# A two-layer hybrid DiT on one core: most adaLN products on VectorE as dot products, and the feed-forward layer's inner features in two parts

## The chip, the cores and the metric

The kernel runs on one core of a Trainium2 chip. The engines are PE (TensorE, matmuls), DVE (VectorE), ACT (ScalarE), POOL (GpSimd) and SP (SyncE, which issues most of the DMAs). The metric is the device time of one execution in microseconds (us), as the median of several; a single profiled execution gives the trace, whose span is a little shorter than that execution's own time.

## The reference, cut to what matters

Two token streams of 256 tokens each (`x` and `ctx`, width 1024) go through two layers. Each layer is a feed-forward sublayer, a mixer (neighbourhood attention and an SSD branch), and a second feed-forward sublayer. In front of every sublayer the stream is normalised, scaled and shifted, and behind it the result is gated, by nine vectors of 1024 features for each layer and stream. These come from one conditioning vector per stream:

```
def adaln(v, w, b):
    m = jax.nn.silu(v) @ w + b          # v: 1024, w: 1024 x 9216
    return m.reshape(m.shape[:-1] + (N_MOD, D_MODEL))

def ffn_sublayer(s, mod, i, g_norm, w_gate, w_up, w_down):
    h = modulate(rmsnorm(s, g_norm), mod[:, :, i], mod[:, :, i + 1])
    return s + 0.5 * mod[:, :, i + 2] * swiglu(h, w_gate, w_up, w_down)   # D_FF = 2816
```

So adaLN is a product of a 1024 x 9216 matrix per layer with just two vectors. Layer 1 needs no second feed-forward and no mixer output for `ctx`.

## The kernel before, in words

**Layout.** Activations lie with features on the partitions and the 512 tokens of both streams (two segments of 256) in the columns. `self.x[k]` holds the residual stream and `self.h[k]` the normalised input of a sublayer, for 128 features each.

**Weights.** Every weight is used as a high and a low half. `wchunk` loads 512 KB (four blocks of 128 rows by 256 columns) into `raw` (3 buffers) with a DMA issued by SP, ACT casts it (L90), and DVE subtracts to get the low half (L91). Both halves lie in `hl` (4 buffers). `gemm_t` then runs three matmuls for each block of 128 rows (L114 to L116).

**Feed-forward.** `ffn` walks over 11 chunks of 256 inner features. A chunk is 96 matmuls, as a rule of 512 columns: two groups of 24 for gate into `pg`, two for up into `pu`. ACT takes Silu of `pg`, DVE multiplies with `pu` (L371), and the product is split into `act` (ACT L303, DVE L304), 22 tiles in all. The four products rotate over three PSUM banks. Chunk 0 goes segment by segment, so that the norm of segment 1 (`norm`, whose `rstd` is a chain of nine tiny DVE operations, L200 to L208, then `dg` at L222, a matmul L224 into `rbc`, and L248 to L252 into `h`) may run beside segment 0's products. After all chunks `onto_x` multiplies `act` with w_down, four blocks of 256 output features, and `resid` (L298) adds each onto `x`. The last `tail` blocks go segment by segment, so that the norm of segment 0 for the next sublayer may run beside segment 1's products.

**adaLN.** One unit is 256 features of one of the nine kinds: two loads of 512 KB into `wa` (issued by SP), and products of `wa` with the 32-column stationary `cs` on PE (L153). Four units share a PSUM bank; DVE copies it (L157), PE sums it with a selection matrix (L160), and DVE adds the bias (L166 and the lines behind it). There are 72 units. The first 8 run in a start phase ahead of the first feed-forward layer. The generator `ada_all` hands out the other 64 in slots between the products of the first three feed-forward layers: 6 kinds in each of layer 0's two, and 4 in layer 1's first.

**Order.** Each engine works through its own instructions in order. A scheduler at build time places the instructions of `ffn`, so the order is fixed by when it expects an operand and an engine to be free. All weight loads and the adaLN loads stand in the one queue that SP issues.

## Time and profile before

| | before |
|---|---|
| median of 3 runs | 2913.41 us (2911.05 to 2914.53) |
| profiled execution | 2915.16 us |
| its span | 2913.2 us |
| PE busy | 2834.8 us (97%) |
| DVE busy | 1699.7 us (58%) |
| ACT busy | 1339.1 us (46%) |

The stages, read from the timeline: the start phase to 26 us, the first feed-forward layer to 447, the mixer of layer 0 with its output projection (the last 50 us of it) to 1318, the second feed-forward layer to 1719, layer 1's first feed-forward layer to 2114, its mixer to 2690, and its second feed-forward layer, for one stream, to the end. The busy times are sums over the whole span; which engine an instruction waits for in one stage is read from windows and from the waits in them.

### The profile page before, as it was taken

The numbers are of one execution on the slowest core, as the hardware profiler recorded it, in microseconds if no ns is written. First come the engines' busy times: TensorE is split into PE (matmuls) and PEld (weight loads), VectorE is DVE, ScalarE is ACT, GpSimd is POOL, SyncE is SP. The second block draws the span as 40 slices with busy tenths as digits, with TensorE's granted clock in tenths as the row PEclk, the third lists the DMA queues.
The fourth block names the chain that finished last, engine by engine and source line by source line (L and its number), as shares of the span: only waits on it lengthen the run. The fifth ranks groups of instructions, "written<-read, shape, count | busy, mean of one in ns | idle before, by whom it ended". The sixth has DMA issues, their size and how long they took to land.

```text
span 2913.2 us, 42876 instructions
## 1 busy us (share of the span) xinstructions
PE 2834.8 (97%) x16872; PEld 2304.1 (79%) x16872; DVE 1699.7 (58%) x3320; ACT 1339.1 (46%) x2447; POOL 76.7 (3%) x132
## 2 busy tenths in 40 slices
PE   7999998999999999999999999999989999999899
PEld 4777788776776777788777797777888787789899
DVE  4333246677569989765333263332477777899654
ACT  3222223544468878733222142222344457787453
POOL 0000000000000000000000000000001000001000
PEclk9999999999999999999999999999999999999999
DMA  7555554322232222344544544444554343235564
GB/s 255 175 155 158 166 167 104 88 55 55 83 87 63 75 74 87 94 155 138 156 145 148 166 152 144 131 145 137 163 145 74 79 127 88 87 109 168 167 188 152
DMA packets 365737, 371.95 MB, mean 128 GB/s; under 512 B 15456, under 2 KB 358624, under 8 KB 365536
## 3 DMA queue, kind: packets, MB, share of 16 engines
q1 hardware_dynamic: 358112, 349.28, 39.7%
q0 software_dynamic: 7424, 19.93, 3.7%
q8 instruction: 133, 2.18, 0.3%
q14 instruction: 68, 0.56, 0.1%
HBM read 360.77 MB, written 8.39 MB: 127 GB/s over the span
## 4 chain that ended last, share of the span: by engine, by line
PE 88%; DVE 5%; DMA 3%; ACT 3%; issue 1%; POOL 0%; SPq 0%; ACTq 0%; DVEq 0%; POOLq 0%
PE pd L114 5%; PE pd L115 5%; PE pd L116 5%; PE pg L114 5%; PE pg L115 5%; PE pg L116 5%; PE pu L114 5%; PE pu L115 5%; PE pu L116 5%; PE xps L114 3%; PE xps L115 3%; PE xps L116 3%; PE ps_y L809 3%; PE ps_ada L153 3%; PE qkps L125 2%; PE qkps L126 2%
## 5 line engine op out<-in xcount | busy, mean ns | idle before, releaser
L91 DVE TENSOR_TENSOR hl<-raw,hl 128x1024 fp32r<-128x1024 f32 (+1 forms) x538 | 625.9, 1166 | 756.9 <-ACT hl L90 756.0
L90 ACT CAST hl<-raw 128x1024 fp32r<-128x1024 f32 (+1 forms) x538 | 538.5, 1003 | 734.9 <-PE pd L116 283.3
L114 PE MATMUL pd<-act,hl 128*128 128x256 f32 (+1 forms) x836 | 280.6, 336 | 0.0
L115 PE MATMUL pd<-act,hl 128*128 128x256 f32 (+1 forms) x836 | 279.6, 334 | 0.0
L116 PE MATMUL pd<-act,hl 128*128 128x256 f32 (+1 forms) x836 | 278.5, 333 | 0.0
L114 PE MATMUL pg<-h,hl 128*128 128x512 f32 (+1 forms) x736 | 267.1, 364 | 6.2 <-ACT h L303 5.0
L115 PE MATMUL pg<-h,hl 128*128 128x512 f32 (+1 forms) x736 | 265.2, 360 | 0.0
L116 PE MATMUL pg<-h,hl 128*128 128x512 f32 (+1 forms) x736 | 264.8, 360 | 0.0
L114 PE MATMUL pu<-h,hl 128*128 128x512 f32 (+1 forms) x696 | 254.7, 366 | 0.0
L115 PE MATMUL pu<-h,hl 128*128 128x512 f32 (+1 forms) x696 | 253.3, 364 | 0.0
L116 PE MATMUL pu<-h,hl 128*128 128x512 f32 (+1 forms) x696 | 252.7, 363 | 0.0
L125 PE MATMUL qkps<-hl,h 128*128 128x256 f32 x672 | 195.5, 291 | 1.8 <-ACT v L453 1.8
L126 PE MATMUL qkps<-hl,h 128*128 128x256 f32 x672 | 193.3, 288 | 0.9 <-DVE hl L91 0.9
L127 PE MATMUL qkps<-hl,h 128*128 128x256 f32 x672 | 192.0, 286 | 0.0
L114 PEld LDWEIGHTS pd<-act,hl 128*128 128x128 f32 x836 | 157.1, 188 | 23.0 <-issue 4.9
L116 PEld LDWEIGHTS pd<-act,hl 128*128 128x128 f32 x836 | 157.0, 188 | 17.0 <-issue 0.8
L115 PEld LDWEIGHTS pd<-act,hl 128*128 128x128 f32 x836 | 157.0, 188 | 16.6 <-issue 1.2
L114 PEld LDWEIGHTS pg<-h,hl 128*128 128x128 f32 x736 | 138.7, 189 | 38.7 <-issue 7.4
L836 DVE SCALAR_TENSOR_TENSOR m<-m,dtn,cbm 128x256 f32<-128x256 f32 (+1 forms) x384 | 144.6, 412 | 36.1 <-ACT m L834 35.6
L115 PEld LDWEIGHTS pg<-h,hl 128*128 128x128 f32 x736 | 139.1, 189 | 23.9 <-DVE h L304 1.3
L116 PEld LDWEIGHTS pg<-h,hl 128*128 128x128 f32 x736 | 139.1, 189 | 23.0 <-issue 0.8
L114 PEld LDWEIGHTS pu<-h,hl 128*128 128x128 f32 x696 | 131.2, 189 | 28.1 <-issue 6.6
(264 smaller groups left out, 5930.8 us busy)
## 6 DMA issues: line engine op xcount, KB each, us to landing
wa<-in_w_ada_dram SPq DMA_DIRECT2D x144, 512.0 KB, 4.6
raw<-in_w_in_dram SPq DMA_DIRECT2D x144, 512.0 KB, 4.0
raw<-in_ffn_w_down_dram SPq DMA_DIRECT2D x95, 512.0 KB, 3.5
raw<-in_ffn_w_gate_dram SPq DMA_DIRECT2D x88, 512.0 KB, 3.8
raw<-in_ffn_w_up_dram SPq DMA_DIRECT2D x88, 512.0 KB, 3.8
raw<-in_ssd_w_o_dram SPq DMA_DIRECT2D x32, 512.0 KB, 3.5
raw<-in_w_out_dram SPq DMA_DIRECT2D x20, 512.0 KB, 3.5
raw<-in_na_w_o_dram SPq DMA_DIRECT2D x16, 512.0 KB, 3.4
```

Source lines behind the costliest of these rows:

```text
L90: nc.scalar.copy(hl[:, 0], t)
L91: nc.vector.tensor_tensor(out=hl[:, 1], in0=t, in1=hl[:, 0].bitcast(F32), op=ALU.subtract)
L114: mm(ps, wh, xh[:, cols], start=(first and i == 0), stop=False)
L115: mm(ps, wh, xl[:, cols], start=False, stop=False)
L116: mm(ps, wl, xh[:, cols], start=False, stop=(last and i == len(st) - 1))
L125: mm(ps, xh[:, cols], wh, start=(i == 0), stop=False)
L126: mm(ps, xh[:, cols], wl, start=False, stop=False)
L127: mm(ps, xl[:, cols], wh, start=False, stop=(i == len(st) - 1))
L153: mm(ps[32 * j : 32 * j + 32, :256], self.cs[:, k0 + j, 6 - 2 * i : 38 - 2 * i], w[:, j], start=(i + k0 == 0), stop=(i == len(units) - 1 a ...
L809: nc.tensor.matmul(*a, **k)
L836: v.scalar_tensor_tensor(out=e[:, o1], in0=e[:, o1], scalar=self.dtn[:, 2 * s + j, r : r + 1], in1=cbm[s][:, d, o1], op0=ALU.mult, op1=ALU ...
```

## The change

The first two kinds of layer 0 stay on PE in the start phase. The other 16 kinds become dot products on DVE: the host transposes their weights (`w_adt`), so that 128 output features lie on the partitions and the 1024 input features in the columns. For each of 8 blocks of a kind, SP loads 512 KB into `wt` (3 buffers), and two `scalar_tensor_tensor` of 128x1024 (one for each stream) multiply it with the broadcast Silu of the conditioning vector (`cb`) and sum along the row (`accum_out`). That makes 128 loads and 256 such operations. At the start of each of the three feed-forward layers, `cb` (1 MB) is loaded and goes through Silu on ACT. The product itself goes to a scratch tile `junk` that nobody reads.

The inner features of a feed-forward layer are used in two parts: after chunk 5 `onto_x` takes the first 12 blocks of `act`, and after chunk 10 the remaining 10, with the last two instead of the last one of the four output blocks going segment by segment. Each part adds onto `x`, so `resid` runs twice for each output block; `act` has 12 buffers in place of 22. The number of matmuls of the feed-forward layers is unchanged. `cc` and `cs` move into a pool that is closed after the start phase.

```
     def ada_all(self):
-        first = [[(0, m, u) for m in (1, 0)] for u in range(4)]
-        rest = [[(l, m, u) for u in range(4)] for l in range(L) for m in range(9)][2:]
-        for units in first + rest:
-            yield from self.ada_steps(units)
...
+        kinds = [(l, m) for l in range(L) for m in range(9)][2:]
+        def load(i):
+            w = self.wada.tile([P, D], F32, name="wt", tag="wt", bufs=3)
+            nc.sync.dma_start(w, self.I["w_adt"][i // KD, i % KD * P : (i % KD + 1) * P, :])
+            return w
+        for i, (l, m) in enumerate(kinds):
+            md = self.mods[9 * l + m][0]
+            for k in range(KD):
+                w = self.wnext or load(i * KD + k)
+                more = not self.stop_after(l, m, k)
+                self.wnext = load(i * KD + k + 1) if more else None
+                for s in range(2):
+                    nc.vector.scalar_tensor_tensor(out=self.junk, in0=w, scalar=1.0, in1=self.cb[:, s], op0=ALU.mult, op1=ALU.mult,
+                                                   accum_out=md[:, k, s : s + 1])
...
-    def onto_x(self, l, m, w, nk, rhs, nseg, tail, ada=None):
+    def onto_x(self, l, m, w, ka, kb, rhs, nseg, tail, ada=None):
...
-            self.wada, self.nwada, self.nada = fp, 2, 1
+            self.wada = fp
+            if nada:
+                self.cb = fp.tile([P, 2, D], F32, name="cb", tag="cb")
+                self.junk = fp.tile([P, D], F32, name="junk", tag="junk")
...
+                nc.scalar.activation(self.cb, self.cb, AF.Silu)
...
-            nsl = 1 + 2 * (nch - 1) + 9
-            slots = iter([4 * nada * (i + 1) // nsl - 4 * nada * i // nsl for i in range(nsl)])
+            half = (nch + 1) // 2
+            nsl = 1 + 2 * (nch - 1) + 12 + 6
+            slots = iter([KD * nada * (i + 1) // nsl - KD * nada * i // nsl for i in range(nsl)])
...
             for c in range(nch):
+                if c == half:
+                    self.after_seg = None
+                    self.onto_x(l, m + 2, wd, 0, 2 * half, actr, nseg, 0, ada)
...
-                    a = fp.tile([P, 2, T], F32R, name="act", tag="act", bufs=KF)[:, :, cols]
+                    a = fp.tile([P, 2, T], F32R, name="act", tag="act", bufs=2 * half)[:, :, cols]
...
-            self.onto_x(l, m + 2, wd, KF, lambda k: (act[k][:, 0], act[k][:, 1]), nseg, 1, ada)
+            self.onto_x(l, m + 2, wd, 2 * half, KF, actr, nseg, 2, ada)
```

What the build-time order makes of it is shown at three places. The first is DVE's queue in a chunk of the first feed-forward layer. Before, one chunk has four weight subtractions (L91), two products (L371), two splits (L304) and sometimes the copy of a finished bank (L157):

```order
L91 TENSOR_TENSOR hl<-raw,hl 128x1024 x2
L371 TENSOR_TENSOR sg<-pu,sg 128x512
L304 TENSOR_TENSOR act<-sg,act 128x512
L91 TENSOR_TENSOR hl<-raw,hl 128x1024
L371 TENSOR_TENSOR sg<-pu,sg 128x512
L91 TENSOR_TENSOR hl<-raw,hl 128x1024
L304 TENSOR_TENSOR act<-sg,act 128x512
L157 COPY adas<-ps_ada 128x256
```

After, the same work stands there (its lines are now L91, L408 and L331), with the dot products (L192) between:

```order
L192 SCALAR_TENSOR_TENSOR junk,mod_3_104<-wt,cb 128x1024 x2
L91 TENSOR_TENSOR hl<-raw,hl 128x1024
L192 SCALAR_TENSOR_TENSOR junk,mod_3_104<-wt,cb 128x1024 x2
L408 TENSOR_TENSOR sg<-pu,sg 128x512
L192 SCALAR_TENSOR_TENSOR junk,mod_3_104<-wt,cb 128x1024
L331 TENSOR_TENSOR act<-sg,act 128x512
L192 SCALAR_TENSOR_TENSOR junk,mod_3_104<-wt,cb 128x1024
L91 TENSOR_TENSOR hl<-raw,hl 128x1024
L192 SCALAR_TENSOR_TENSOR junk,mod_3_104<-wt,cb 128x1024
L408 TENSOR_TENSOR sg<-pu,sg 128x512
L91 TENSOR_TENSOR hl<-raw,hl 128x1024
L331 TENSOR_TENSOR act<-sg,act 128x512
```

Twelve or thirteen dot products stand in each chunk from 1 to 5, and eight in each of the four w_down blocks of the first part; from chunk 6 on none are left in the feed-forward layers of layer 0 (96 operations in each), and none in layer 1's first (64).

The second place is DVE's queue where the norm of segment 1 ahead of the second feed-forward layer of layer 0 is worked out. Before, the nine steps of the reciprocal root stand in one piece, followed by `dg`:

```order
L200 TENSOR_SCALAR rs_a<-ssq 128x2
L201 TENSOR_SCALAR rs_y<-rs_a 128x2
L202 TENSOR_TENSOR rs_t<-rs_y 128x2
L203 TENSOR_TENSOR rs_t<-rs_t,rs_a 128x2
L204 SCALAR_TENSOR_TENSOR rs_y<-rs_t,rs_y 128x2
L205 SCALAR_TENSOR_TENSOR rs_t<-rs_y 128x2
```

After, a dot product of this layer's kinds stands behind nearly every step (the steps are now L227 to L235, `dg` is L249):

```order
L227 TENSOR_SCALAR rs_a<-ssq 128x2
L192 SCALAR_TENSOR_TENSOR junk,mod_8_109<-wt,cb 128x1024
L228 TENSOR_SCALAR rs_y<-rs_a 128x2
L192 SCALAR_TENSOR_TENSOR junk,mod_8_109<-wt,cb 128x1024
L229 TENSOR_TENSOR rs_t<-rs_y 128x2
L192 SCALAR_TENSOR_TENSOR junk,mod_8_109<-wt,cb 128x1024
L230 TENSOR_TENSOR rs_t<-rs_t,rs_a 128x2
L192 SCALAR_TENSOR_TENSOR junk,mod_8_109<-wt,cb 128x1024
L231 SCALAR_TENSOR_TENSOR rs_y<-rs_t,rs_y 128x2
L192 SCALAR_TENSOR_TENSOR junk,mod_8_109<-wt,cb 128x1024
```

Eight dot products have moved between `rs_a` and `dg` there, and one between `dg` and the normalised tiles; 11 more stand in the output projection ahead of it.

The third place is SP's queue in a chunk of the first feed-forward layer. Before, two `wa` loads stand among the four raw loads of a chunk (two of gate, two of up):

```order
L83 DMA wa<-in_w_ada_dram 128x4x256 x2
L83 DMA raw<-in_ffn_w_gate_dram 128x4x256
L83 DMA raw<-in_ffn_w_up_dram 128x4x256
L83 DMA wa<-in_w_ada_dram 128x4x256 x2
L83 DMA raw<-in_ffn_w_up_dram 128x4x256
L83 DMA raw<-in_ffn_w_gate_dram 128x4x256
```

After, six or seven `wt` loads of the same size stand among them:

```order
L83 DMA raw<-in_ffn_w_gate_dram 128x4x256 x2
L182 DMA wt<-in_w_adt_dram 128x1024 x4
L83 DMA raw<-in_ffn_w_up_dram 128x4x256
L182 DMA wt<-in_w_adt_dram 128x1024
L83 DMA raw<-in_ffn_w_up_dram 128x4x256
L182 DMA wt<-in_w_adt_dram 128x1024 x2
```

The loads of a feed-forward layer's kinds have moved into its first half, where a raw load now stands behind up to four `wt` loads.

## Rows read from the trace of the kernel before

**Rows 1.** The page's first part: PE, its busy time, share and instructions

```profile
PE 2834.8 (97%) x16872; PEld 2304.1 (79%) x16872; DVE 1699.7 (58%) x3320; ACT 1339.1 (46%) x2447; POOL 76.7 (3%) x132
```

**Rows 2.** Windows: stretch, its length, busy time by engine, PEclk, DMA share, GB/s

```profile
0.00:26.00 26.00, 11.51 (x84) 6.13 (x84) 12.63 (x38) 12.72 (x20) 0.20 (x4) 0.97 0.96 318
61.00:311.00 250.00, 250.00 (x1261) 191.35 (x1260) 82.50 (x113) 69.87 (x102) 0.00 (x0) 1.00 0.53 161
```

**Rows 3.** Lines by form, PE: adaLN products, count, busy us, mean ns, idle before

```profile
L153 PE MATMUL ps_ada<-wa,cs 128*32 128x256 f32 x1152 | 82.8, 391 | 0.1
```

**Rows 4.** Timeline of PE around one adaLN unit: start, duration, instruction

```profile
149.70 0.40 PE L116 MATMUL pg<-h,hl 128*128 128x512 f32 x1
...
152.50 0.40 PE L116 MATMUL pg<-h,hl 128*128 128x512 f32 x1
...
158.10 0.40 PE L116 MATMUL pu<-h,hl 128*128 128x512 f32 x1
158.42 1.07 PE L153 MATMUL ps_ada<-wa,cs 128*32 128x256 f32 x16
...
159.76 0.40 PE L115 MATMUL pu<-h,hl 128*128 128x512 f32 x1
```

**Rows 5.** Timeline of PE around one selection matmul group

```profile
194.10 0.40 PE L116 MATMUL pg<-h,hl 128*128 128x512 f32 x1
194.33 0.51 PE L160 MATMUL ps_ada<-c_cst,adas 128*128 128x8 f32 x4
...
195.24 0.39 PE L116 MATMUL pg<-h,hl 128*128 128x512 f32 x1
```

**Rows 6.** Lines by form, DVE: weight subtraction, and operations with two float32 sources

```profile
L91 DVE TENSOR_TENSOR hl<-raw,hl 128x1024 fp32r<-128x1024 f32 x483 | 589.2, 1222 | 710.4 <-ACT hl L90 709.5
L836 DVE SCALAR_TENSOR_TENSOR m<-m,dtn,cbm 128x256 f32<-128x256 f32 x192 | 92.0, 479 | 36.1 <-ACT m L834 35.6
L836 DVE SCALAR_TENSOR_TENSOR m<-m,dtn,cbm 128x128 f32<-128x128 f32 x192 | 66.1, 344 | 0.0
```

**Rows 7.** Timeline of DVE: two independent operations in a row

```profile
64.25 1.22 DVE L91 TENSOR_TENSOR hl<-raw,hl 128x1024 fp32r<-128x1024 f32 x1
65.38 1.28 DVE L304 TENSOR_TENSOR act<-sg,act 128x512 fp32r<-128x512 f32 x2
```

**Rows 8.** Timeline of ACT: an operation with an accumulator, and its read

```profile
559.63 0.70 ACT L518 ACTIVATE p<-ps_s,mx 128x512 f32<-128x512 f32 x1
560.21 0.20 ACT L518 ACTIVATION_READ_ACCUMULATOR p<-ps_s,mx 128x1 f32 x1
560.30 0.69 ACT L518 ACTIVATE p<-ps_s,mx 128x512 f32<-128x512 f32 x1
```

**Rows 9.** Timeline of DVE: segment 1's norm ahead of layer 0's second feed-forward

```profile
1325.18 0.16 DVE L200 TENSOR_SCALAR rs_a<-ssq 128x2 f32<-128x2 f32 x1 [2.38 <-PE ssq L217]
...
1326.95 0.48 DVE L222 TENSOR_SCALAR dg<-c_cst,rs_y 128x128 f32<-128x128 f32 x2
...
1329.29 1.27 DVE L252 SCALAR_TENSOR_TENSOR h<-nh,mod,h 128x256 fp32r<-128x256 f32 x3
```

**Rows 10.** Timeline of PE there: the first matmul of segment 1

```profile
1330.28 0.28 PE L114 MATMUL pg<-h,hl 128*128 128x256 f32 x1
```

**Rows 11.** Timeline of PE behind an idle time: 19 matmuls from 467.67 to 471.65

```profile
466.82 1.20 PE L224 MATMUL rbc<-dg,ones 128*128 128x128 f32 x4 [10.40 <-DVE dg L222]
467.67 0.56 PE L125 MATMUL qkps<-hl,h 128*128 128x256 f32 x1
...
471.65 0.28 PE L125 MATMUL qkps<-hl,h 128*128 128x256 f32 x1
```

**Rows 12.** Waits from 61 to 311 us: who waits for whom, total, times, longest

```profile
ACT hl L90 <- PE pu L116: 40.8, 19, 3.1
DVE sg L371 <- PE pu L116: 35.5, 20, 2.9
```

**Rows 13.** DMA issues of the page: count, KB each, median us to landing

```profile
wa<-in_w_ada_dram SPq DMA_DIRECT2D x144, 512.0 KB, 4.6
```

More of the change, by code (lines that the diff above doesn't have):

```diff
@@ L150, in ada_steps @@
                 w = self.wada.tile([P, 4, 256], F32, name="wa", tag="wa", bufs=self.nwada)
[L151 removed]
+                self.load(w, self.I["w_ada"], k0, 4, m * D + u * 256, 256)
                 for j in range(4):
@@ L173, in ada_all @@
-    def ada_all(self):
-        first = [[(0, m, u) for m in (1, 0)] for u in range(4)]
-        rest = [[(l, m, u) for u in range(4)] for l in range(L) for m in range(9)][2:]
-        for units in first + rest:
-            yield from self.ada_steps(units)
-            self.ada_done = units[0][:2]
-            if self.pause:
+            if m == 1:
+                nc.vector.scalar_tensor_tensor(out=md, in0=md, scalar=1.0, in1=two(PAR["g1"][0] + 2 * u), op0=ALU.add, op1=ALU.mult)
+    def ada_all(self):
+        for u in range(4):
+            yield from self.ada_steps([(0, m, u) for m in (1, 0)])
+            yield
+        self.ada_done = (0, 1)
+        nc = self.nc
+        kinds = [(l, m) for l in range(L) for m in range(9)][2:]
[12 more added lines that the diff above has]
+                                                   accum_out=md[:, k, s : s + 1])
+                if k == KD - 1:
+                    two = lambda n, o: self.pars[l][:, PAR[n][0] + o : PAR[n][0] + o + KD][:, :, None].to_broadcast([P, KD, 2])
+                    nc.vector.tensor_tensor(out=md, in0=md, in1=two("b_ada", m * KD), op=ALU.add)
+                    if m in (1, 4, 7):
+                        nc.vector.scalar_tensor_tensor(out=md, in0=md, scalar=1.0, in1=two({1: "g1", 4: "gm", 7: "g2"}[m], 0),
+                                                       op0=ALU.add, op1=ALU.mult)
+                    elif m in (2, 8):
+                        nc.vector.tensor_scalar(out=md, in0=md, scalar1=0.5, scalar2=None, op0=ALU.mult)
+                    self.ada_done = (l, m)
@@ L180, in ada_all, with stop_after @@
                 yield
+    def stop_after(self, l, m, k):
+        return k == KD - 1 and (l, m) in ((0, 7), (1, 4), (1, 8))
     def mod(self, l, m, k, s):
-        return self.mods[9 * l + m][k // 2][:, k % 2, s : s + 1]
+        return self.mods[9 * l + m][1][k // 2][:, k % 2, s : s + 1]
     def fill(self, n=1):
@@ L312, in onto_x @@
                 continue
-            if ada and split:
-                ada(True)
             for sg in [[s] for s in range(nseg)] if split else [list(range(nseg))]:
@@ L318, in onto_x @@
                     pd = [self.bank("pd")[:, : len(sg) * SEG] for _ in range(2)]
-                    for a in range(0, nk, 4):
-                        ws = self.wcols(w, min(4, nk - a), cc * 256, k0=a)
+                    for a in range(ka, kb, 4):
+                        ws = self.wcols(w, min(4, kb - a), cc * 256, k0=a)
                         for t in range(2):
-                            self.gemm_t(pd[t], ws, t * P, P, rhs, cols, a == 0, a + 4 >= nk)
-                        if ada and not split and a % 8:
+                            self.gemm_t(pd[t], ws, t * P, P, rhs, cols, a == ka, a + 4 >= kb)
+                        if ada and not split:
                             ada()
@@ L335, in ffn @@
         with tc.tile_pool(name="ffn", bufs=1) as fp, tc.tile_pool(name="pph", bufs=1, space=PSUM) as self.pph:
-            self.wada, self.nwada, self.nada = fp, 2, 1
+            self.wada = fp
+            if nada:
+                self.cb = fp.tile([P, 2, D], F32, name="cb", tag="cb")
+                self.junk = fp.tile([P, D], F32, name="junk", tag="junk")
+                nc.sync.dma_start(self.cb.rearrange("p s k -> p (s k)"),
+                                  self.I["c2"].rearrange("s k -> (s k)")[None, :].to_broadcast([P, 2 * D]))
+                nc.scalar.activation(self.cb, self.cb, AF.Silu)
             act = []
             nch = DFF // 256
-            nsl = 1 + 2 * (nch - 1) + 9
-            slots = iter([4 * nada * (i + 1) // nsl - 4 * nada * i // nsl for i in range(nsl)])
+            half = (nch + 1) // 2
+            nsl = 1 + 2 * (nch - 1) + 12 + 6
+            slots = iter([KD * nada * (i + 1) // nsl - KD * nada * i // nsl for i in range(nsl)])
             def ada(end=False):
-                self.pause = end
-                self.fill(1 if end and nada else next(slots, 0))
+                self.fill(KD * nada if end else next(slots, 0))
+            actr = lambda k: (act[k][:, 0], act[k][:, 1])
             for c in range(nch):
+                if c == half:
+                    self.after_seg = None
+                    self.onto_x(l, m + 2, wd, 0, 2 * half, actr, nseg, 0, ada)
                 if pre and c == 0:
@@ L1004, in body @@
                 if l == 0 and m < 2:
-                    K.mods.append([cp.tile([P, 2, 2], F32, name=f"mod{m}_{u}") for u in range(4)])
+                    K.mods.append((None, [cp.tile([P, 2, 2], F32, name=f"mod{m}_{u}") for u in range(4)]))
                 else:
-                    t = cp.tile([P, 4, 2, 2], F32, name=f"mod{l}_{m}")
-                    K.mods.append([t[:, u] for u in range(4)])
+                    t = cp.tile([P, KD, 2], F32, name=f"mod{l}_{m}")
+                    K.mods.append((t, [t[:, 2 * u : 2 * u + 2] for u in range(4)]))
         K.pars = [cp.tile([P, NPAR], F32, name=f"par{l}") for l in range(L)]
-        nc.sync.dma_start(cc, I["cc"])
         K.load_con("cst", cp)
```

26 lines of the change are left out of this document (12 added, 14 removed).

## The prediction

> **What bounds the kernel now.** I read the engine line first [rows 1]: PE is busy 97% of the span, DVE 58%. That is an average, so I then read the windows of the stages that the change touches. From 61 to 311 us, inside the first feed-forward layer, PE is busy in all of its 250 us and DVE in 82.5 [rows 2], a third. The reader is to see there that every microsecond of PE work which leaves such a stage shortens it, as long as the work that takes its place fits into DVE's other two thirds. The waits of the same stretch say what DVE and ACT do meanwhile: ACT's weight casts wait for PE to give back a weight buffer (19 waits, 40.8 us), and DVE's product waits for PE's `pu` (20 waits, up to 2.9 us) [rows 12]. Both run ahead of PE. The start phase is the opposite: 318 GB/s with the DMA engines busy 0.96 of the time, and PE busy 11.5 of 26 us [rows 2]; the change leaves its work as it is.
>
> **What PE loses.** The adaLN products are 1152 recorded matmuls, 16 for each of 72 units [rows 3]. Their mean of 391 ns is no price, since they overlap. I take it from the timeline. Two 512-column matmuls of the same kind stand 12 places apart at 149.70 and 152.50, so one place is 0.233 us [rows 4]. Around one unit the starts go from 158.10 to 159.76, 1.66 us, with two ordinary places in it: 1.66 - 2 x 0.233 = 1.19 us for a unit. For a selection group it is 195.24 - 194.10 = 1.14 us with three ordinary places: 0.44 us [rows 5]. 64 units and 16 groups leave: 64 x 1.19 + 16 x 0.44 = 76.2 + 7.0 = **83.2 us**. All of it lies in the three feed-forward layers, where PE is the bound. The two-part sum over inner features costs PE nothing in itself, since the matmuls are the same in number.
>
> **What DVE gains: the price of one dot product.** No operation of DVE with an accumulator is in the trace, so I bound it. Multiplications of the same form with two float32 sources take 479 ns for 256 columns and 344 for 128 [rows 6]: 1.055 ns a column, hence 479 + 768 x 1.055 = 1.29 us for 1024. An independent operation starts before the one ahead has ended: 1.22 us long, but the next start 1.13 later [rows 7], so 1.29 becomes a pitch of 1.20. That is the lower end, an accumulator that costs nothing. A dependent operation follows later: nine steps of the root take 1326.95 - 1325.18 = 1.77 us, 0.197 each for a duration of 0.16 [rows 9], 0.04 more than the duration. Two dot products in a row both write `junk` and so wait for one another: 1.33. ACT's accumulator is read by an instruction of its own, which makes the pitch 0.09 longer: 0.70 us long, the next start 0.67 later, where its read starts after 0.58 (559.63, 560.21, 560.30 in [rows 8]). With that the upper end is 1.42. I take the middle, **1.35 us**, as the order has both pairs in a row and single ones between other work. 256 x 1.35 = 346 us of DVE, in stages where it has more than twice that free; but the order puts them in the first halves.
>
> [...]
>
> **Does it fit?** In chunks 1 to 5 the order gives DVE 12 or 13 dot products, four subtractions (1.13 each) and four operations of 0.6 [rows 7]: 13 x 1.35 + 4.5 + 2.4 = 24.5 us, against PE's 96 x 0.233 = 22.4. With 1.20 it would be 22.5, just even; with 1.42 it is 25.4. So DVE falls behind by 0 to 3 us a chunk, 0 to 15 over five chunks. In the w_down blocks of the first part it is about even (72 x 0.233 = 16.8 us of PE; 8 x 1.35 + 3 x 1.13 + 4 x 0.48 = 16.1 of DVE). PE doesn't notice at once: the four products of a chunk rotate over three banks, so DVE's reading of a bank may come two products late, 2 x 24 x 0.233 = 11.2 us. The upper end thus exceeds the cover by 4 us in each of layer 0's two layers; layer 1's first has 64 dot products, about 10 a chunk, and fits. There is a second path: an SP queue in order, in which a raw load stands behind up to four `wt` loads, and each of these waits for one of three buffers that only DVE frees. Whenever DVE is late, the next raw load is late too, and a load takes 4.6 us to land [rows 13]. I charge one and a half landings for each of layer 0's two layers and one half for layer 1's: 3.5 x 4.6 = 16, an estimate, and take **+15 us** for both paths. Ends: 0, if the cover holds; 40, if it fails from the first chunk (two layers x 5 x 3, and half as much for layer 1's and the queue). All other DVE work of the change is small: 16 additions of 128x16, and 40 additions onto `x` of 0.48 [rows 6], beside 16.8-us blocks; the copies of adaLN banks go.
>
> **Where it can't fit: the norm of segment 1.** Ahead of layer 0's second feed-forward layer, PE needs segment 1's `h` at 1330.28 [rows 10], and the first one is being written from 1329.29 [rows 9], about 0.6 us of slack. The order now has eight dot products between `rs_a` and `dg`. Nothing else is queued on PE between segment 0's products and `rbc`, which waits for `dg`. So the chain grows by 8 x 1.35 less the gaps they fill (some 0.3), 10.5 us; the ninth hides mostly under `rbc`. Less 0.6 it is 9.9. Behind an idle time of 10.4 us PE ran 19 matmuls of 256 columns in 3.98 us instead of 19 x 0.117 = 2.2 [rows 11]: 1.8 more. Sum **+12 us**. The ends are 9 (at 1.20) and 13.
>
> **Smaller terms.** Eleven dot products in the output projection are 15 us of DVE, one of them in the root chain of segment 0's norm, with `cb` and its Silu beside them: **+2.5** (0 to 8). The start of the first feed-forward layer, where 1 MB of `cb` (two landings like those of rows 13) joins transfers that were at 318 GB/s [rows 2], 3 us at that rate: **+2** (0 to 5). The turn from w_down back to chunk 6, where PE's next bank waits for `resid`: **+2** (0 to 4, two operations of 0.48 in each of three layers and what they wait for). The blocks that go by segment are now two of 10 in place of one of 22, so what covers the norm of segment 0 falls from 132 to 120 matmuls of half the columns, 15.5 to 14.1 us: nothing, or 1.4 in each of two layers if the cover was just long enough.
>
> **The sum.** -83.2 + 15 + 12 + 2.5 + 2 + 2 = -49.7. The profiled run (2915.2, span 2913.2) lies 1.8 above the median of the three, 2913.4; from the median this is **2864 us**. About 0.2% (6 us) is what a measurement of this kernel can tell from no change.
>
> **The rivals.** *The cover holds.* DVE's price is at the lower end or its lateness stays inside 11.2 us, and only the norm and the turn cost: -83.2 + 9 to 12 + 2 = 2841, 2835 to 2850. For it: DVE and ACT wait for PE now [rows 12]. Against it: the order fills DVE to the brim.
>
> *The queue binds.* DVE is at 1.42 and SP's queue passes its lateness to the raw loads: 40 in place of 15, so 2889, 2880 to 2905. If it takes yet 20 more, the gain is spent, and the time is within 0.2%.
>
> [...]
>
> **How the numbers follow.** Forecast 0.47; cover holds 0.18; queue binds 0.20; within 0.2% 0.03; half rate 0.12. Own range of the forecast 2848 to 2882. The range reaches from 2838, which holds most of the first rival, to 2905, the end of the queue's: 0.47 + 0.15 + 0.20, about 8 in 10. Faster by over 0.2% is 0.47 + 0.18 + 0.20 = 0.85, within it 0.03, slower 0.12.
>
> **What the profile after would show.** Right: no `ps_ada` matmuls behind the start phase, PE's busy time down by about 83 us, dot products of 1.29 us (plus a second short instruction) at a pitch of 1.3 to 1.4, PE idle for some 10 us before `rbc` at the second feed-forward layer, and idle times of PE in chunks 3 to 5 and the first w_down blocks, released by DVE's `hl` or by a bank. Wrong: dot products of over 2 us (half rate), or PE without any idle time in the first halves (cover holds), or idle times of which the releaser is a DMA (queue).

## The result, and the profile after

The changed kernel takes 2844.9 us (median; 2843.8 to 2852.3), against 2914.0 us for the kernel before on the same chip: a ratio of 0.9769 (95% interval 0.9757 to 0.9780), 69 us faster. That lies inside the predicted range (2838 to 2905) but not inside the forecast's own (2848 to 2882). It is the time of the first rival, the cover that holds (2835 to 2850); the predicted range reached down to 2838 to hold most of that rival.

The page's first part of the changed kernel answers to [rows 1]:

```profile
PE 2752.6 (97%) x15748; PEld 2274.6 (80%) x15748; DVE 2007.0 (71%) x3793; ACT 1344.2 (47%) x2453; POOL 76.9 (3%) x132
```

PE has lost 82 us of busy time (2834.8 before), the span 69.2 (2913.2 before, 2844.0 after, both of the profiled executions). DVE has gained 307. The lines by form say where PE's loss comes from; they answer to [rows 3] (columns: line, engine, operation, shapes, count; then busy us and mean ns; then idle time before):

```profile
L153 PE MATMUL ps_ada<-wa,cs 128*32 128x256 f32 x128 | 11.2, 426 | 0.0
...
L160 PE MATMUL ps_ada<-c_cst,adas 128*128 128x8 f32 x16 | 2.1, 242 | 0.5 <-DVE adas L157 0.5
```

Of 72 units the 8 of the start phase are left, 128 recorded matmuls in place of 1152. What takes their place on DVE is a `scalar_tensor_tensor` and, as an instruction of its own, the accumulator's read (lines by form, DVE; the second row is other work, an addition of 256 columns):

```profile
L192 DVE SCALAR_TENSOR_TENSOR junk<-wt,cb 128x1024 f32<-128x1024 f32 x256 | 312.5, 1221 | 7.8 <-DMA wt<-in_w_adt_dram 3.4 <-ACT cb L367 0.2
...
L263 DVE TENSOR_TENSOR ssacc<-ssacc,sst 128x256 f32<-128x256 f32 x99 | 41.3, 419 | 2.8 <-ACT sst L262 1.4
...
L192 DVE DVE_READ_ACCUMULATOR junk<-wt,cb 128x1 f32 x256 | 20.8, 81 | 0.0
```

One dot product lasts 1.22 us, and its read 0.08. The prediction's extrapolation had 1.29.

Where the 69 us went is read by stage. The bounds are the starts of the first matmul of each stage in PE's timeline, in the profiled executions, in us:

| stage | before | after | difference |
|---|---|---|---|
| start phase, to the first gate product | 26.3 | 25.6 | -0.7 |
| layer 0's first feed-forward layer | 419.5 | 386.7 | -32.8 |
| mixer of layer 0 | 823.0 | 822.9 | -0.1 |
| output projection, second feed-forward layer, layer 1's first | 844.0 | 804.9 | -39.1 |
| mixer of layer 1 | 570.5 | 571.6 | +1.1 |
| last projection and last feed-forward layer | 223.0 | 224.5 | +1.5 |
| end | 6.9 | 7.8 | +0.9 |

By the prediction's prices the first feed-forward layer should lose 24 x 1.19 + 6 x 0.44 = 31.2 us of PE, and it lost 32.8. The fourth row should lose 40 x 1.19 + 10 x 0.44 = 52.0 and lost 39.1: 12.9 us stayed there.

The windows say why the first layer lost all of it (columns as in [rows 2]: stretch, length, busy time of PE, PEld, DVE, ACT, POOL, then PEclk, DMA share and GB/s). They are its chunks 1 to 5, its first part of w_down, and its chunks 6 to 10:

```profile
61.00:176.00 115.00, 115.00 (x507) 93.00 (x506) 112.26 (x173) 39.29 (x68) 0.00 (x0) 1.00 0.79 255
176.00:243.00 67.00, 67.00 (x289) 54.27 (x288) 60.48 (x97) 13.15 (x13) 0.00 (x0) 1.00 0.66 207
243.00:355.00 112.00, 112.00 (x481) 90.18 (x480) 36.92 (x40) 31.11 (x39) 0.00 (x0) 1.00 0.30 90
```

In chunks 1 to 5 DVE is busy 112.3 of 115 us, and PE all the same 115 of 115. The forecast's idle times of PE aren't there.

DVE falls behind a little, though. Its first product of three successive chunks (timeline of DVE, start and duration) starts at:

```profile
126.05 0.68 DVE L408 TENSOR_TENSOR sg<-pu,sg 128x512 f32<-128x512 f32 x1
...
148.95 0.69 DVE L408 TENSOR_TENSOR sg<-pu,sg 128x512 f32<-128x512 f32 x1
...
171.93 0.69 DVE L408 TENSOR_TENSOR sg<-pu,sg 128x512 f32<-128x512 f32 x1
```

22.90 and 22.98 us apart, against 22.4 of PE: DVE loses half a microsecond a chunk, 3 us over five chunks, where by the prediction's estimate 11.2 us may be lost. The waits from 61 to 243 us answer to [rows 12]:

```profile
ACT hl L90 <- PE pd L116: 45.4, 10, 4.5
ACT act L330 <- DVE sg L408: 25.8, 6, 5.6
...
ACT hl L90 <- DMA raw<-in_ffn_w_gate_dram: 2.4, 1, 2.4
...
DVE sg L408 <- PE pu L116: 0.3, 1, 0.3
```

In [rows 12] DVE's product waited 20 times for PE's `pu`, 35.5 us in all, in a stretch that is a third longer. Of that wait 0.3 us are left, once: DVE now comes after PE. But PE itself is in no row of the list; it waits for nobody. ACT's casts still wait for PE, and the loads held them up once, for 2.4 us.

### The profile page after: what moved, and what is told of

Its sections match the earlier page's. It is cut to its first block, busy times and chain, and to the rows that moved or that the text cites. A ratio compares the mean times of both kernels' runs of the same rounds, so it can differ in the third digit from the quotient of the medians.

```text
span 2844.0 us, 41229 instructions
## 1 busy us (share of the span) xinstructions
PE 2752.6 (97%) x15748; PEld 2274.6 (80%) x15748; DVE 2007.0 (71%) x3793; ACT 1344.2 (47%) x2453; POOL 76.9 (3%) x132
## 4 chain that ended last, share of the span: by engine, by line
PE 85%; DVE 6%; DMA 4%; ACT 3%; issue 1%; POOL 0%; SPq 0%; ACTq 0%; DVEq 0%; POOLq 0%
PE pg L115 5%; PE pg L114 5%; PE pg L116 5%; PE pd L116 5%; PE pd L115 5%; PE pd L114 5%; PE pu L115 5%; PE pu L116 5%; PE pu L114 5%; PE xps L114 3%; PE xps L115 3%; PE xps L116 3%; PE ps_y L846 3%; PE qkps L125 2%; PE qkps L127 2%; PE qkps L126 2%
## 5 line engine op out<-in xcount | busy, mean ns | idle before, releaser
L91 DVE TENSOR_TENSOR hl<-raw,hl 128x1024 fp32r<-128x1024 f32 (+1 forms) x538 | 624.1, 1162 | 468.0 <-ACT hl L90 466.5
L192 DVE SCALAR_TENSOR_TENSOR junk<-wt,cb 128x1024 f32<-128x1024 f32 x256 | 312.5, 1221 | 7.8 <-DMA wt<-in_w_adt_dram 3.4
L116 PE MATMUL pd<-act,hl 128*128 128x512 f32 (+1 forms) x824 | 277.3, 336 | 0.0
L115 PE MATMUL pd<-act,hl 128*128 128x512 f32 (+1 forms) x824 | 276.6, 336 | 0.0
L114 PE MATMUL pd<-act,hl 128*128 128x512 f32 (+1 forms) x824 | 276.1, 335 | 0.0
L115 PEld LDWEIGHTS pd<-act,hl 128*128 128x128 f32 x824 | 154.8, 188 | 18.1
L114 PEld LDWEIGHTS pd<-act,hl 128*128 128x128 f32 x824 | 154.9, 188 | 17.9
L116 PEld LDWEIGHTS pd<-act,hl 128*128 128x128 f32 x824 | 155.0, 188 | 16.5
```

The lines of the kernel that those rows point to most:

```text
L91: nc.vector.tensor_tensor(out=hl[:, 1], in0=t, in1=hl[:, 0].bitcast(F32), op=ALU.subtract)
L114: mm(ps, wh, xh[:, cols], start=(first and i == 0), stop=False)
L115: mm(ps, wh, xl[:, cols], start=False, stop=False)
L116: mm(ps, wl, xh[:, cols], start=False, stop=(last and i == len(st) - 1))
L192: nc.vector.scalar_tensor_tensor(out=self.junk, in0=w, scalar=1.0, in1=self.cb[:, s], op0=ALU.mult, op1=ALU.mult, accum_out=md[:, k, s : s ...
```

## The experiments

The theory after the result: the 83 us of adaLN matmuls are gone in full; inside the chunks the dot products cost nothing, since DVE has just the time for them; what is lost again is lost in the norm of segment 1 at layer 0's second feed-forward layer. The rivals: the two parts of the inner features gave or took some of it; the transfers cost; or DVE is late after all and PE pays somewhere else.

### No dot product in the norm, nor in the output projection ahead of it

The place is seen in PE's timeline of the changed kernel, with the idle time before each instruction in brackets:

```profile
1286.28 0.50 PE L114 MATMUL pg<-h,hl 128*128 128x256 f32 x2 [1.54 <-ACT h L278]
...
1303.91 1.19 PE L251 MATMUL rbc<-dg,ones 128*128 128x128 f32 x4 [5.51 <-DVE dg L249]
1306.21 0.80 PE L114 MATMUL pg<-h,hl 128*128 128x256 f32 x2 [1.11 <-ACT h L278]
```

and in DVE's, which answers to [rows 9]:

```profile
1293.21 0.15 DVE L227 TENSOR_SCALAR rs_a<-ssq 128x2 f32<-128x2 f32 x1
1293.28 1.21 DVE L192 SCALAR_TENSOR_TENSOR junk<-wt,cb 128x1024 f32<-128x1024 f32 x1
1294.42 0.08 DVE L192 DVE_READ_ACCUMULATOR junk<-wt,cb 128x1 f32 x1
1294.42 0.16 DVE L228 TENSOR_SCALAR rs_y<-rs_a 128x2 int32<-128x2 int32 x1
...
1303.48 0.48 DVE L249 TENSOR_SCALAR dg<-c_cst,rs_y 128x128 f32<-128x128 f32 x2
```

From `rs_a` to `dg` it is 10.27 us, against 1.77 in [rows 9]. Nearly every step of the root now stands behind a dot product and its read. PE stands still for 5.5 us before `rbc`, which wants `dg`, then 1.1 us for the first `h`, and the matmuls between and behind go at a lower granted clock for a while: `rbc`'s matmuls take 1.19 us, against 0.68 in the second profile of `late_cb`, where PE had not stood still, and those of 256 columns behind them start 0.21 us apart up to 1310 us and 0.12 from there on. The granted clock is 0.50 up to 1310 us, and 1.00 in the window from 1312 to 1320:

```profile
1303.90:1310.00 6.10, 4.98 (x21) 4.69 (x22) 6.06 (x16) 2.62 (x6) 0.00 (x0) 0.50 0.46 156
```

The first line of PE's timeline above is an idle time of 1.5 us ahead of segment 0's first product. Three more lie in the output projection before it, where the 11 dot products stand: 0.75 and 0.54 us for `x`, 0.82 us for a sum of the norm. All `rbc` waits of the whole program together, by the waits of PE, are:

```profile
PE rbc L251 <- DVE dg L249: 14.7, 4, 5.5
```

so 5.5 us at this place is also the longest of them.

The experiment lets the Silu that fills `cb` wait for the first product of chunk 0, in the two layers that begin with a norm of their own. In layer 0's second one that moves 20 dot products out of the output projection and the norm, into the chunks; so it takes both places away at once:

```
-                nc.scalar.activation(self.cb, self.cb, AF.Silu)
+                if pre:
+                    nc.scalar.activation(self.cb, self.cb, AF.Silu)
...
                 if c == 0:
+                    if nada and not pre:
+                        z = self.sm.tile([P, 1], F32, name="zero", tag="zero")
+                        nc.vector.tensor_scalar(out=z, in0=y[:, :1], scalar1=0.0, scalar2=None, op0=ALU.mult)
+                        nc.scalar.activation(self.cb, self.cb, AF.Silu, bias=z)
                     ada()
```

> The changed kernel, but in layer 0's second and layer 1's first feed-forward layer the Silu that fills cb waits for the first product of chunk 0, so no dot product can stand in the output projection or in the norm of segment 1; all of the work is still done. Theory (the dot products cost only where they stand between the steps of that norm; elsewhere DVE's free time holds them): PE's 5.5 us of idle time before rbc, the 1.5 and 1.1 beside it and the lower clock behind them go, some 11 us: 2834 us (2831 to 2837). Rival 1 (the lost 12 us come from the transfers of cb and wt beside the output projection or from the order of the last blocks, not from DVE's chain): 2841 to 2846. Rival 2 (the 85 dot products that move into the chunks no longer fit there): 2845 or more.

Measured: 2839.2 us (2837.4 to 2842.8), ratio to the kernel before 0.9746 (0.9730 to 0.9762). The direction is the theory's, the size is half of it, between the theory's range and rival 1's. So it was run again, beside the unedited changed kernel on the same chip:

> The changed kernel once more, unedited, beside the next two on the same chip: 2844 to 2847, as the ground for their difference.

> The kernel of late_cb once more, with more rounds, since its stage of the second feed-forward layer was 9.5 us shorter and its median only 6: theory (the norm's chain is the only place where dot products cost) 8 to 11 us below the unedited kernel beside it, 2834 to 2838. Rival (some of it comes back in the mixers): 5 to 7 below, 2838 to 2841.

Measured: the unedited kernel 2845.5 us (0.9766, 0.9752 to 0.9779), `late_cb` again 2837.7 (0.9738, 0.9725 to 0.9751): 7.7 us less, between the 8 to 11 of the theory and the 5 to 7 of the rival. In the profile of the second the chain is as it was before the change (DVE's timeline):

```profile
1291.53 0.16 DVE L227 TENSOR_SCALAR rs_a<-ssq 128x2 f32<-128x2 f32 x1 [0.79 <-PE ssq L244]
...
1293.30 0.48 DVE L249 TENSOR_SCALAR dg<-c_cst,rs_y 128x128 f32<-128x128 f32 x2
```

1.77 us from `rs_a` to `dg`. The windows of the output projection and of chunk 0 show PE almost without idle time (46.9 of 47 us and 23.8 of 24) and at a granted clock of 1.00:

```profile
1236.00:1283.00 47.00, 46.88 (x297) 41.97 (x296) 30.14 (x58) 19.61 (x31) 4.32 (x8) 1.00 0.71 234
1283.00:1307.00 24.00, 23.84 (x197) 23.23 (x196) 18.52 (x48) 10.86 (x19) 0.00 (x0) 1.00 0.21 62
```

What the dot products cost at these two places can be read from PE's timeline, from the first product of the output projection over segment 0's first product to the first product of chunk 1. In the changed kernel the three are at 1235.22, 1286.28 (above) and 1319.38, in the second profile of `late_cb` as follows:

```profile
1235.22 0.40 PE L114 MATMUL pd<-h,hl 128*128 128x512 f32 x1
...
1319.38 0.40 PE L114 MATMUL pg<-h,hl 128*128 128x512 f32 x1
```

```profile
1236.73 0.39 PE L114 MATMUL pd<-h,hl 128*128 128x512 f32 x1
...
1283.36 0.28 PE L114 MATMUL pg<-h,hl 128*128 128x256 f32 x1
...
1307.98 0.40 PE L114 MATMUL pg<-h,hl 128*128 128x512 f32 x1
```

| us | output projection | chunk 0 with the norm | both |
|---|---|---|---|
| changed kernel | 51.06 | 33.10 | 84.16 |
| changed kernel again | 51.18 | 32.76 | 83.94 |
| `late_cb` | 46.65 | 24.63 | 71.28 |
| `late_cb` again | 46.63 | 24.62 | 71.25 |
| `no_dots` (below) | 46.61 | 24.63 | 71.24 |

The dot products thus cost 4.4 us in the output projection and 8.5 in the norm, 12.9 together, as much as stayed in the fourth row. The chunks into which they moved are no longer for it: from the first matmul of chunk 1 to the last of chunk 5 it takes 111.8 us in the changed kernel, in `late_cb` and in `no_dots`. Rival 1 and rival 2 are out for this stage.

By stage, the fourth row of the table above takes 795.4 and 796.4 us in the two profiles of `late_cb`, 804.9 and 805.9 in the two of the changed kernel: 9.5 us less, both times, and not 12.9. What comes back lies in the w_down blocks, and dot products have no part in it. Two windows inside layer 1's first part of w_down, at a granted clock of 1.00 and with PE busy throughout, the changed kernel first and `late_cb` second, hold 220 and 217 matmuls:

```profile
1810.00:1860.00 50.00, 50.00 (x220) 41.03 (x219) 16.29 (x21) 9.45 (x9) 0.00 (x0) 1.00 0.31 96
```

```profile
1800.00:1850.00 50.00, 50.00 (x217) 40.54 (x216) 20.78 (x31) 9.45 (x9) 0.00 (x0) 1.00 0.31 94
```

From one start to the next it is 0.229 us in the one and 0.232 in the other; in the second parts of the first three feed-forward layers it is 0.114 to 0.115 against 0.119 us for 256 columns. `no_dots`, without any dot product, has 0.233 in this first part too. Over all w_down blocks that makes some 5 us, an estimate from these distances and the counts of matmuls; 1.3 of them are seen at the end of the first feed-forward layer (387.9 and 388.4 us for it, against 386.7 and 386.9). Why the same matmuls are slower in `late_cb` wasn't isolated. The mixers and the last layer vary by 2 to 4 us between executions of one and the same kernel (mixer of layer 1: 571.6 and 569.8 in the changed kernel; mixer of layer 0: 826.2 and 823.6 in `late_cb`), so that what lies there is not settled.

### The floor: no dot products at all

```
-                w = self.wnext or load(i * KD + k)
...
-                for s in range(2):
-                    nc.vector.scalar_tensor_tensor(out=self.junk, ...)
+                if k == 0:
+                    nc.vector.memset(md, 0.0)
```

> The changed kernel with all 256 dot products, their loads and cb left out (the 16 kinds are zero plus bias): the floor without adaLN work in the feed-forward layers. Theory: the same as late_cb within 3 us, 2831 to 2836, since only the norm's chain costs. Rival (the dot products and their 64 MB of loads also slow PE's weights in the chunks or at the start): clearly lower, 2820 or less.

Measured: 2833.8 us (2830.4 to 2837.9), ratio 0.9730 (0.9716 to 0.9745). This kernel leaves the 16 kinds at zero plus bias. All 256 dot products, their 64 MB of loads and `cb` together thus cost 2844.9 - 2833.8 = 11 us. The rival's 2820 is out. `late_cb` is 4 to 5 us above it (2837.7 and 2839.2 against 2833.8), where the theory had at most 3 between them. That isn't a price of dot products in the chunks: in the fourth row it takes 794.7 us, 0.7 to 1.7 less than `late_cb`, in the first feed-forward layer 388.2, as `late_cb`; the rest lies in mixers and the last layer, which hold no dot product.

### The two parts alone

The kernel before, with adaLN on PE, got the two parts and the two last blocks by segment:

```
+                if c == half:
+                    self.after_seg = None
+                    self.onto_x(l, m + 2, wd, 0, 12, actr, nseg, 0, ada)
...
-            self.onto_x(l, m + 2, wd, KF, lambda k: (act[k][:, 0], act[k][:, 1]), nseg, 1, ada)
+            self.onto_x(l, m + 2, wd, 12, KF, actr, nseg, 2, ada)
```

> The kernel before (adaLN on PE) with the feed-forward layers in two parts of 12 and 10 blocks and the last two output blocks by segment. Theory: the two parts give and cost almost nothing, 2913 (2909 to 2916), as PE has the same matmuls; the whole gain is adaLN's. Rival: the shorter idle times at the start of the mixers (8.8 in place of 10.4 us, 7.9 in place of 8.3) are the split's and it gives 3 to 6 us by itself: 2907 to 2910; or the second additions onto x cost: 2917 or more.

Measured: 2918.8 us (2917.7 to 2921.8), ratio 1.0022 (1.0013 to 1.0032). The two parts cost 5.5 us by themselves; they bring nothing but the room in SBUF. The theory's "almost nothing" falls, and so does the rival's gain; the rival's other case, 2917 or more, has the time. By stage, in its profiled execution (2917.7, the lowest of ten, 2.5 us above that of the kernel before), the first feed-forward layer is 0.6 us longer, the fourth row 2.0 and the last 1.1: some 3.7 in four layers, with 1.6 less in the start phase, 0.8 less in layer 0's mixer and 1.2 more in layer 1's. Of the 2.0 us, 1.8 are two waits of PE in chunk 0 of layer 1's first feed-forward layer, which the kernel before doesn't have:

```profile
1720.33 0.39 PE L114 MATMUL pu<-h,hl 128*128 128x256 f32 x1 [0.80 <-DVE x L298]
...
1721.79 0.50 PE L116 MATMUL pg<-h,hl 128*128 128x256 f32 x2 [0.96 <-DVE hl L91]
```

They stand in the changed kernel too (0.75 and 0.96 us), and in `late_cb` and `no_dots`. At the turn from w_down back to chunk 6 PE has no wait of over 0.1 us in the changed kernel. Where the rest of the 5.5 us lies wasn't isolated. With this, the price of adaLN on PE can be read from two kernels that are alike in the parts and differ in adaLN (its matmuls, its loads, and DVE's share): 2918.8 - 2833.8 = 85 us, against the 83.2 worked out.

To see whether the cost can be had back where no room is needed, the last feed-forward layer, which has no dot products, got one part again, on top of `late_cb` and two scratch tiles:

```
-                if c == half:
+                if nada and c == half:
...
-            self.onto_x(l, m + 2, wd, 2 * half, KF, actr, nseg, 2, ada)
+            self.onto_x(l, m + 2, wd, 2 * half if nada else 0, KF, actr, nseg, 2 if nada else 1, ada)
```

> late_cb with two scratch tiles, and with the last feed-forward layer, which has no dot products, in one part as before the change. Theory (the two parts cost 1 to 2 us in each layer by their second additions onto x and the turn, 5.5 in all): 1 to 2 below late_cb. Rival (their cost lies elsewhere, in the starts of the mixers): the same as late_cb within 0.5 us.

Measured: 2839.4 us (2837.1 to 2843.0), ratio 0.9747 (0.9733 to 0.9760), against 2837.7 for `late_cb` beside it. The theory's 1 to 2 us of gain aren't there. The last layer, for one stream, takes 225.6 us in both profiles.

### One block by segment in place of two

```
-            self.onto_x(l, m + 2, wd, 2 * half, KF, actr, nseg, 2, ada)
+            self.onto_x(l, m + 2, wd, 2 * half, KF, actr, nseg, 1, ada)
```

> The changed kernel with one output block by segment in the second part in place of two. Theory: segment 0's norm takes some 13 us from its first root step to its last h, and one block of 10 gives it 60 matmuls of 256 columns, 7.1 us, in place of 14.1: PE then waits some 5 to 6 us at the end of three feed-forward layers, +12 to +18: 2857 to 2863. Rival (that norm is not what PE waits for there, since PE idles for segment 1's anyway and one wait takes the place of the other): 2843 to 2848.

Measured: 2854.9 us (2851.1 to 2857.4), ratio 0.9801 (0.9786 to 0.9816): 10 us more than the changed kernel, a little under the 12 to 18 expected. But the time doesn't lie where the theory has it. PE's timeline at the end of the first feed-forward layer does show waits for segment 0's norm (the second line is already in the mixer):

```profile
413.62 0.68 PE L251 MATMUL rbc<-dg,ones 128*128 128x128 f32 x4 [1.42 <-DVE dg L249]
...
422.47 0.58 PE L125 MATMUL qkps<-hl,h 128*128 128x256 f32 x1 [4.31 <-ACT h L278]
```

With a third of 1.37 us between, that is 7.1 us; in the changed kernel the `rbc` of segment 0 stands at 405.19 there without any wait. Yet the layer and the mixer behind it together take 1206.2 us, against 1209.6 in the changed kernel, and PE's idle time in that mixer is 19.7 us, against 23.5: nothing is lost there, as one wait takes the place of another, which is what the rival says. What is lost is lost in the fourth row (820.6 us, 15.7 more; the mixer behind it is 4.4 shorter), and 13 of it at the turn from layer 0's second to layer 1's first feed-forward layer. There the order of `tail1` puts nine dot products between the steps of segment 1's norm, where the changed kernel has none (timelines of DVE and of PE):

```profile
1674.50 0.16 DVE L227 TENSOR_SCALAR rs_a<-ssq 128x2 f32<-128x2 f32 x1 [0.71 <-PE ssq L244]
...
1685.88 0.48 DVE L249 TENSOR_SCALAR dg<-c_cst,rs_y 128x128 f32<-128x128 f32 x2
```

```profile
1686.30 1.19 PE L251 MATMUL rbc<-dg,ones 128*128 128x128 f32 x4 [6.90 <-DVE dg L249]
```

11.4 us from `rs_a` to `dg`, against 1.77 in the changed kernel (1673.27 to 1675.04), and PE waits 6.9 us. So this experiment repeats the finding of the first one at a second place. Whether one block of 10 covers segment 0's norm it doesn't settle: waits for it are there, but ahead of a mixer they cost nothing in the sum.

### Is DVE's lateness paid by PE?

> The changed kernel with three dot products for each block in place of two (the first stream's twice, with the same result): 128 more, about 156 us more of DVE. The order still puts 13 in each chunk and carries the rest into chunks 6 to 8. Theory (what counts is whether DVE's free time in the whole stage holds them; PE doesn't notice): 2845 to 2850. Rival (the predicted reason, DVE falls behind once the chunks are full and takes PE's weights with it): 2860 to 2885.

```
-                for s in range(2):
+                for s in (0, 1, 0):
```

Measured: 2843.7 us (2840.7 to 2848.4), ratio 0.9757 (0.9741 to 0.9774), the same as the changed kernel, and a little under the theory's 2845 to 2850. 128 more dot products, half as many again, cost nothing that can be told. The windows of the first feed-forward layer, to be read beside those of the changed kernel above:

```profile
61.00:176.00 115.00, 115.00 (x507) 92.96 (x506) 112.52 (x171) 38.60 (x67) 0.00 (x0) 1.00 0.65 207
176.00:243.00 67.00, 67.00 (x289) 54.27 (x288) 64.65 (x105) 13.15 (x13) 0.00 (x0) 1.00 0.60 190
243.00:355.00 112.00, 112.00 (x482) 90.17 (x481) 88.04 (x131) 31.44 (x39) 0.00 (x0) 1.00 0.48 148
```

Chunks 1 to 5 are as full as before (112.5 us), for the order puts no more there; the rest went into chunks 6 to 10, where DVE rises from 36.9 to 88.0 of 112 us. PE is busy in all of it. The layer thus had room for half as many again, and the prediction's reason for a loss, a DVE that falls behind and takes PE's weights with it, doesn't happen. A DVE that is later than the cover of 11.2 us wasn't tried, as the order fills no chunk further.

### What a dot product costs

The changed kernel's pairs look like this in DVE's timeline:

```profile
120.09 1.22 DVE L192 SCALAR_TENSOR_TENSOR junk<-wt,cb 128x1024 f32<-128x1024 f32 x1
121.24 0.08 DVE L192 DVE_READ_ACCUMULATOR junk<-wt,cb 128x1 f32 x1
121.36 1.22 DVE L192 SCALAR_TENSOR_TENSOR junk<-wt,cb 128x1024 f32<-128x1024 f32 x1
122.51 0.08 DVE L192 DVE_READ_ACCUMULATOR junk<-wt,cb 128x1 f32 x1
122.51 1.22 DVE L91 TENSOR_TENSOR hl<-raw,hl 128x1024 fp32r<-128x1024 f32 x1
```

A dot product behind another starts 1.27 us after it (120.09, 121.36); other work starts 1.15 us after it (121.36, 122.51), at the very moment when the accumulator's read starts. Two experiments take the 0.12 us apart. The first uses two scratch tiles in turn:

```
-                    nc.vector.scalar_tensor_tensor(out=self.junk, in0=w, ...
+                    nc.vector.scalar_tensor_tensor(out=self.wada.tile([P, D], F32, name="junk", tag="junk", bufs=2), in0=w, ...
```

> The changed kernel with two scratch tiles in turn in place of one, so that a dot product doesn't wait for the one before to have written. If the 0.12 us between the accumulator's read and the next dot product is that wait, the pitch of a pair falls from 1.27 to about 1.15; if it is the accumulator itself, it stays 1.27. The time is the same within 2 us either way if the cover holds.

```profile
119.53 1.22 DVE L192 SCALAR_TENSOR_TENSOR junk<-wt,cb 128x1024 f32<-128x1024 f32 x1
120.67 0.08 DVE L192 DVE_READ_ACCUMULATOR junk<-wt,cb 128x1 f32 x1
120.67 1.22 DVE L192 SCALAR_TENSOR_TENSOR junk<-wt,cb 128x1024 f32<-128x1024 f32 x1
...
121.82 1.22 DVE L91 TENSOR_TENSOR hl<-raw,hl 128x1024 fp32r<-128x1024 f32 x1
```

The pitch falls to 1.14 and 1.15, with the accumulator's read still there. The second leaves the accumulator out:

```
-                    ... op0=ALU.mult, op1=ALU.mult, accum_out=md[:, k, s : s + 1])
+                    ... op0=ALU.mult, op1=ALU.mult)
```

> The changed kernel with the dot products' sums left out (the products are computed and not summed, the 16 kinds are zero plus bias). If the accumulator costs only a short instruction of its own, each product stays 1.22 us and the read of 0.08 goes; if it halved anything, the product gets shorter. The time is the same within 2 us if DVE's price isn't what PE waits for, save the norm's chain: up to 1 us less.

```profile
122.54 2.48 DVE L194 SCALAR_TENSOR_TENSOR junk<-wt,cb 128x1024 f32<-128x1024 f32 x2
```

Two products with one scratch tile take 2.48 us from the first's start to the second's end, that is a pitch of 1.26 if the second lasts 1.22, without any read. From the start of such a pair to that of the other work behind it are 2.39 us here (122.54 to 124.93), and 2.42 with the accumulator (120.09 to 122.51 above). So the 0.12 us are the wait for the scratch tile that the one before has written, and the accumulator adds at most 0.03 us to a pair. The times of these two, one execution each, were 2851.2 and 2851.4 us, 6 above the changed kernel's median, where "the same within 2 us" was expected, and within its spread (up to 2852.3). Nothing on the time follows from them.

## Why the prediction was right or wrong

**What bounds the kernel, and what PE loses: right.** 83.2 us were worked out; PE's busy time fell by 82.2, and the two kernels in two parts, with adaLN on PE and without adaLN, differ by 85.0. Taking the price of a unit from the starts of its neighbours, and not from the 391 ns of one matmul, was what made it so.

**The price of a dot product: the step that failed first.** 1.35 us was taken between 1.20 and 1.42. Measured are 1.15 with other work behind and 1.27 with another dot product behind, so about 1.2, the low end. Two of its three parts were wrong. The duration was extrapolated from operations with the same form but a scalar read from memory (479 ns for 256 columns), where an addition of 256 columns takes 419; the dot product has a constant, and 1.22 us is the duration of a plain subtraction of 1024 columns [rows 6]. That the scalar from memory makes those 60 ns is the author's estimate and wasn't shown. And the accumulator's read was charged with 0.09 by ACT's example [rows 8]; on DVE a next instruction that doesn't write `junk` starts with it (both at 122.51 above). The third part, the wait for `junk`, was real and was 0.12, about as charged (1.33 - 1.20).

**Does it fit: the term that failed by it.** This is where the forecast went wrong: +15 us was charged for a DVE that falls behind by 2 us a chunk, and the runs show none of it (PE busy 115 of 115 us in chunks 1 to 5, and the same 111.8 us there in layer 0's second layer with and without dot products). At the true price DVE falls behind by 0.5 us a chunk (22.9 against 22.4), inside the 11.2 us of cover that were worked out. The text had the case in its own sum ("With 1.20 it would be 22.5, just even") and gave it to the rival with 0.18. The path through SP's queue, priced with one and a half landings, showed as a single wait of 2.4 us of an ACT that had time. Not only was the price too high: `dots_three` shows that the layer holds half as many dot products again, so the picture of a DVE at the brim of a whole layer was wrong as well; only five of ten chunks are full. That the time lies in the stated range is owed to that range's low end, not to the mechanism of the forecast.

**The norm of segment 1: right in place and mechanism, too large in size.** +12 was charged, 8.5 measured. The chain grew by 8.5 us (1.77 to 10.27), where 10.5 was expected, for the same reason of price. And PE had more to do meanwhile than 0.6 us: in the kernel before, 20 of segment 0's 96 matmuls still stood behind `rbc` (1327.38 us, up to segment 1's first at 1330.28 [rows 10]); in the changed kernel's order all 96 run ahead of it.

```profile
1327.38 0.68 PE L224 MATMUL rbc<-dg,ones 128*128 128x128 f32 x4
```

20 x 0.118 = 2.4 us, and with them and the 0.6 a chain 8.5 us longer leaves a wait of 5.5, as measured. The 1.1 us for `h` and some 2 us of lower clock make up the rest (an estimate from PE's timeline: `rbc`'s matmuls 0.5 us longer, and 14 matmuls in 2.99 us from 1307.02 to 1310.01, where 0.118 each make 1.65). That the change moved work into the gaps of a dependent chain was to be seen in the order alone.

**The smaller terms.** For the dot products in the output projection +2.5 was charged, and they cost 4.4. For the start of the first layer +2 was charged; that layer lost its full 31 us. The two parts were said to cost nothing but 2 us for the turns; by themselves they cost 5.5 (1.0022, 1.0013 to 1.0032), and the part of it that was found isn't at the turn back to chunk 6 but in chunk 0 of layer 1's first layer. Two blocks by segment were counted as enough; the changed kernel's `rbc` of segment 0 waits for nothing at the end of the first layer, but `tail1` doesn't show that the second block is needed.

Put together from the stages: -83.2 for adaLN, +12.9 for the dot products in the output projection and the norm, and +1.7 (the waits found) to +5.5 for the two parts make -69 to -65, and -69 was measured. Against the predicted sum the lag is about 0 in place of 15, the norm with the output projection 12.9 in place of 14.5, the start of the first layer about 0 in place of 2, and the two parts up to 5.5 in place of 2. The lag alone is most of the 19 us between 2864 and 2845.

**The rivals.** No run shows the half rate (a dot product of over 2 us), to which the prediction gave 0.12: the dot product reads two float32 sources, writes its accumulator, and lasts 1.22 us, as long as a subtraction of two tiles without an accumulator (1.222 us [rows 6]), and a pair of them takes 2.42 us to the start of other work behind it, against 2.39 without the sums (`no_accum`). With its accumulator it is two instructions on DVE in this trace: `DVE_READ_ACCUMULATOR`, 81 ns in the mean, 256 times. The queue that binds is out by `no_dots`: with all the loads left out as well, only 11 us are gained, and those lie elsewhere; and by `dots_three`, which has more work for DVE and takes no longer.

## What to carry to other kernels

Where one engine was busy in every microsecond of a stage (PE, 250 of 250 us) and another in a third of it (DVE, 82.5), moving a small product across paid its full pitch on the first: 83.2 us by the pitches, and 82.2 of PE's busy time gone. Before charging for the second, add up its work over the whole stage and ask how many microseconds late it may be; being at 98% in a stretch (112.3 of 115 us) cost nothing here. What cost was cover work that a scheduler slipped between the steps of a short dependent chain on which the busy engine waits, at two places in two kernels (PE waited 5.5 us for `dg` in the changed kernel, 6.9 in `tail1`): let such work depend on something that comes after the chain. And compare two kernels at the place of the edit before comparing their times; here 12.9 us were won at the place and 7.7 in the time, and slower matmuls elsewhere hide some 5, by the estimate from their distances.

## What the runs showed of the hardware that was not expected

An accumulated sum on VectorE was free in pitch: 1.14 to 1.15 us from one 128x1024 float32 dot product to the next, with its 0.08 us read between, when they wrote to different scratch tiles (`junk2`), against 1.13 behind a subtraction of that size [rows 7]. One scratch tile for all cost 0.12 us at each pair, for a result that nobody reads. The w_down matmuls of 512 columns followed one another at 0.229 us in some stretches and at 0.232 to 0.233 in others, of one kernel (the changed one: 0.229 from 1810 to 1850 us, 0.233 from 178 to 241) or of two, with PE busy throughout and a granted clock of 1.00 in both; why is open. And the best version run here that does all the work, `late_cb`, at 2837.7 us, differs from the changed kernel by a few lines that only delay a Silu.
